# Block 1 of a two-block network on one Trainium2 core: where its modulation sums, token shift, norm weights and low weight parts are computed

## The chip, the cores and the metric

The kernel runs on one core of a Trainium2 chip. A core has TensorE for matrix products (PE in the profile, its weight loads PEld), VectorE (DVE), ScalarE (ACT), GpSimd (POOL), and SyncE (SP), which here issues most DMA transfers. Each engine takes its instructions strictly in its own order and waits on semaphores for the others. The metric is the device time of one execution in microseconds (us), the median of the runs.

## The reference, cut to what matters

Two blocks are computed on 512 tokens of 1024 channels, all in fp32. The change lies in the first; the second (attention, two MLPs, a gated recurrence) follows it and is not touched.

```
mod = silu(c) @ w_ada + b_ada              # shift, scale, gate
h = x * (1 + scale) + shift
p = h @ w_in
# branch A: u, v, gate = parts of p
v = layer_norm(gelu(v), ln_v_g, ln_v_b)    # per token, in 8 groups of 64 channels
v = einsum('gts,bcsgd->bctgd', w_m, v) + b_spatial   # mixes 128 tokens, causal
out_a = gelu(u) * v * silu(gate)
# branch B: r, k, v, gate, decay and rate inputs
p_b = p_b + mu * (prev_token(p_b) - p_b)   # token shift
... rwkv7 recurrence over 512 tokens, group norm, * silu(gate)
o = concat([out_a, out_b]) @ w_out
x = layer_norm(ALPHA * x + gate * o, ln_g, ln_b)
```

## The kernel before, in words

Every large product is made of three products of fp32r halves: a weight `raw` is cast to its upper part `wh` on ScalarE and the rest, `wl = raw - wh`, is subtracted (`wsplit`, L173); activations are split likewise into `aH` and `aL`. One chunk of output channels is then 8 steps of three matmuls (`mm3`, L181: the weight's and the activation's upper parts, and the two mixed products), 24 matmuls of 128x512 in all, summed in one PSUM bank.

Block 1 has three stages.

The **start loop** (L396 to L421) goes over eight chunks of input channels. For chunk k it forms shift and scale: `ada_acc` (L349) multiplies eight blocks of `w_ada` by silu(c) and adds them into two accumulators in turns (steps 0 and 1 start them, 2 to 7 add, step 8 adds the two), `modulated` (L379) sums the result over partitions with two matmuls against a column of ones, adds the bias into `mod`, turns x and applies them: ScalarE writes `h`, then its upper part `aH`, then `xa`, the scaled x for later. VectorE subtracts `aL`. TensorE multiplies chunk k with six blocks of `w_in`. The block is inside `ordered()`: each engine issues these elementwise instructions in the order of the program, and the matmuls have an order token too. The sums of chunk k+1 are formed while chunk k is multiplied.

The **mixing stage** runs a list written out by hand, `ORDER` (L41): products for k (`k`) and r (`r`) of four pairs of heads, `prep` in parts (`g`), the norm (`n`), transposed weights (`t`) and mixing (`m`) of branch A, the window products `lmat` (`l`), and steps of filling products (`f`). This order fixes TensorE's instructions; the elementwise instructions of the other engines are placed by a list scheduler with priorities. Two PSUM banks carry `mm`, three `sm`, two `mg`, one `po`. A product can start only when an older one has left its bank, and leaves it through `shift_evac` (L431): ScalarE copies the bank to `sh`, GpSimd subtracts neighbouring tokens, VectorE combines them with `mu`.

In the **inverse and window stage** VectorE inverts 32x32 blocks in 62 small dependent instructions (`inverse`, L742; `TV` and `bz` in the rows), the result goes through DRAM (`scT`), and eight windows of the recurrence follow, each starting with a product that needs it (`mg<-Tst,M`). TensorE fills the time of the inverse with the eight products of `ugate` (L654).

`pow_` (L242, shown as L245) is a power on GpSimd that all norms use.

Of the kernel before, what the change touches and what calls it, by code (L numbers as in the profile page):

```python
# [48 lines left out]
class Acts:  # L49
    """Channel-major activations split exactly into two float32r parts."""  # L50
# [11 lines left out]
class Kern:  # L62
# [30 lines left out]
    def psums(self, tags, keep=0):  # L93
        """PSUM banks, so many for each tag; the first pools may stay"""
# [62 lines left out]
    def wload(self, src, k, m, eng=None):  # L157
        """src: DRAM [k*128, m] -> raw tile view [128, k, m]"""
# [31 lines left out]
    def gemm(self, w, col0, acts, K, evac, idx, m=P, leng=None, tag="mm"):  # L190
        """one chunk of m output channels: psum[m, T] = w[:, col0:col0+m].T @ acts"""
# [9 lines left out]
    def gemm_halves(self, w, cols, acts, K, evac, idxs, then=None, tags=None):  # L201
        """chunks of output channels, the first half of the tokens of all of them before the second"""
# [10 lines left out]
    def split(self, src, hi, lo, g=None):  # L213
        """hi + lo = src * g, exactly split; src fp32 in SBUF"""
# [8 lines left out]
    def tokstat(self, acc_list, s=FULL, tag="sm"):  # L223
        """acc tiles [128, T] -> psum [128 tok, len * blocks] of the sums over partitions"""
# [7 lines left out]
    def bcast(self, *cols, tag="sm"):  # L232
        """[128 tok, blocks] each -> psum [128, blocks * 128] each, the same on every partition"""
# [14 lines left out]
    def consts(self):  # L248
# [22 lines left out]
                ("ln_g", r1("ln_g"), 8), ("ln_b", r1("ln_b"), 8)],  # L271
# [5 lines left out]
    def params(self, tag, rows_tile):  # L277
        """parameters, channel on partition: their loads and what turns them"""
# [22 lines left out]
    def block1(self):  # L301
# [10 lines left out]
        mod = self.cp.tile([P, 24], F32, tag="mod", name="mod")  # shift, 1 + scale, gate  # L312
# [6 lines left out]
        # what the output projection and its norm need again waits in DRAM  # L319
# [21 lines left out]
        def ada_load(pool, k, lo, n, bufs):  # L341
            """n blocks of w_ada, lo * 8 + k, (lo + 1) * 8 + k, .."""
# [6 lines left out]
        def ada_acc(acc, raw, steps=range(9)):  # L349
# [46 lines left out]
        with self.ordered():  # L396
            self.petoken = "start"
            ada_acc(cur[3], cur[1])
            w_ = self.wsplit(cur[2], 1, 6 * P, nc.gpsimd)
            h32 = modulated(0, cur[0], cur[3])  # L400
            for k in range(8):
                wh, wl = w_
                if k < 7:
                    cur = load(k + 1)
                    ada_acc(cur[3], cur[1], range(AS))
                self.tt(hL[k], h32, self.f(hH[k]), ALU.subtract)
                if k < 7:
                    ada_acc(cur[3], cur[1], range(AS, 9))
                for f in loads[2 * k : 2 * k + 2]:
                    f()  # L410
                for tb in range(NB):
                    s = slice(tb * P, (tb + 1) * P)
                    self.mm3(psv[tb], hH[k][:, s], hL[k][:, s], wh[:, 0, :T], wl[:, 0, :T], k == 0, k == 7)
                    if tb == SB and k < 7:
                        w_ = self.wsplit(cur[2], 1, 6 * P, nc.gpsimd)
# [26 lines left out]
        mk2 = b([P, 2, RC], "mk2")  # columns t of A (s < t) and of R (s <= t); rows s twice  # L442
# [5 lines left out]
        # rows (head, s), columns (head, t): s in the lower, t in the upper half of one head  # L448
# [6 lines left out]
        # -------- B branch: low-rank inputs of decay and in-context rate  # L455
# [3 lines left out]
        k00 = self.tl(pp, [P, T], "k0")  # L459
# [4 lines left out]
        hp = b_([P, 16], "hp")  # w0/2, a0/2, k_a/2, 1-k_a/2  # L464
# [6 lines left out]
        nc.gpsimd.memset(m64[:, :, 0:1], 0.0)  # L471
        ind2 = b_([P, 2], "ind2")
# [5 lines left out]
        def k_gemm(p):  # L478
            ks[p] = self.tl(pp, [P, T], "k0")
# [7 lines left out]
        def prep(p):  # L487
            """what a pair of heads brings to the windows, in parts that other products may come between"""
# [16 lines left out]
            nc.gpsimd.tensor_copy(out=PCt[p], in_=eP[:, :, RC])  # L505
# [1271 lines left out]
```

## Time and profile before

| | |
|---|---|
| median of 3 runs | 1627.69 us (1627.19 to 1629.02) |
| span of the profiled execution, first to last instruction | 1623.7 us |
| the profiled execution's own time | not recorded apart from its span; the median is 4.0 us above the span |
| TensorE, VectorE, ScalarE, GpSimd busy | 1554.1, 947.0, 704.4, 325.0 us |
| mean granted TensorE clock | 0.987 |

A row of the timeline gives the start in us, the time in us that the row's instructions cover, engine, line, operation, the tile written and the tiles read, shapes and types, the count, and in brackets how long the engine had been idle and what it waited for. An fp32 matmul against ones is two rows of the trace. A granted clock of 1.00 is the 2.4 GHz level, 0.50 the 1.2 GHz level.

### The profile page before, as it was taken

How to read it: one execution, taken by the hardware profiler on the slowest of the kernel's cores; microseconds unless marked ns; L12 is line 12 of the kernel's file. 1: busy time of each engine (PE TensorE's matmuls, PEld its weight loads, DVE VectorE, ACT ScalarE, POOL GpSimd, SP SyncE). 2: the span in 40 equal slices, each digit the busy share in tenths (PEclk: the TensorE clock that was granted, in tenths of full speed). 3: DMA queues.
4: the chain of work that ended last, by engine and by line, in shares of the span. 5: the costliest groups of instructions: out<-in, count | busy, mean ns of one | idle time of the engine just before them, and what ended most of it. 6: DMA issues, size and time to landing. Idle time of an engine off the chain costs nothing. (4 is left out here: it accounts for less than half of the span.)

```text
span 1623.7 us, 22045 instructions
## 1 busy us (share of the span) xinstructions
PE 1554.1 (96%) x8389; PEld 1317.7 (81%) x8389; DVE 947.0 (58%) x1651; ACT 704.4 (43%) x1217; POOL 325.0 (20%) x459
## 2 busy tenths in 40 slices
PE   5987979999999999999999999999999999999998
PEld 4766768889978899888888887888889988888886
DVE  7798595678667738233343456677754824343445
ACT  3533315655666645332232334666535523322331
POOL 4465631234310023000000032222313200000000
PEclk9998889999999999999999999999999999999999
DMA  9732445544123133333333232322213223231421
GB/s 290 219 96 82 75 130 144 176 139 112 52 69 91 33 111 90 93 92 102 91 93 102 80 102 66 103 66 66 71 47 105 91 79 115 64 120 65 120 88 52
DMA packets 272894, 161.70 MB, mean 100 GB/s; under 512 B 29465, under 2 KB 253316, under 8 KB 272788
## 3 DMA queue, kind: packets, MB, share of 16 engines
q1 hardware_dynamic: 271492, 157.33, 33.6%
q0 software_dynamic: 1152, 2.70, 0.5%
q8 instruction: 66, 1.08, 0.3%
q14 instruction: 40, 0.33, 0.1%
q10 hardware_dynamic: 144, 0.26, 0.1%
HBM read 147.42 MB, written 11.53 MB: 98 GB/s over the span
## 5 line engine op out<-in xcount | busy, mean ns | idle before, releaser
L123 DVE TENSOR_TENSOR wl<-raw,wh 128x1024 fp32r<-128x1024 f32 (+2 forms) x228 | 272.1, 1194 | 291.1 <-ACT wh L140 287.0
L140 ACT CAST wh<-raw 128x1024 fp32r<-128x1024 f32 (+3 forms) x244 | 242.6, 996 | 449.1 <-PE mm L143 354.2
L143 PE MATMUL mm<-bL,wh 128*128 128x512 f32 (+1 forms) x752 | 282.6, 378 | 1.0 <-DVE bL L133 1.0
L143 PE MATMUL mm<-bH,wl 128*128 128x512 f32 (+1 forms) x752 | 281.5, 377 | 0.0
L143 PE MATMUL mm<-bH,wh 128*128 128x512 f32 (+1 forms) x752 | 278.9, 378 | 0.1
L143 PE MATMUL mm<-aH,wh 128*128 128x512 f32 (+1 forms) x656 | 240.6, 369 | 11.2 <-DVE gt L133 7.0
L143 PE MATMUL mm<-aH,wl 128*128 128x512 f32 (+1 forms) x656 | 236.8, 362 | 1.5 <-DVE wl L123 1.5
L143 PE MATMUL mm<-aL,wh 128*128 128x512 f32 (+1 forms) x656 | 237.7, 363 | 0.0
L143 PEld LDWEIGHTS mm<-bL,wh 128*128 128x128 f32 x752 | 141.1, 188 | 29.0 <-DVE bL L133 1.8
L143 PEld LDWEIGHTS mm<-bH,wl 128*128 128x128 f32 x752 | 141.1, 188 | 27.4
L143 PEld LDWEIGHTS mm<-bH,wh 128*128 128x128 f32 x752 | 139.1, 188 | 28.4 <-ACT hg_vt L137 0.5
L143 PEld LDWEIGHTS mm<-aH,wh 128*128 128x128 f32 x656 | 125.1, 191 | 33.4 <-DVE gt L133 7.9
L143 PEld LDWEIGHTS mm<-aH,wl 128*128 128x128 f32 x656 | 125.1, 191 | 20.7 <-DVE wl L123 1.9
L143 PEld LDWEIGHTS mm<-aL,wh 128*128 128x128 f32 x656 | 125.5, 191 | 18.3 <-issue 0.7
L143 PE MATMUL mm<-wh,aH 128*128 128x512 f32 x288 | 113.5, 396 | 1.5 <-ACT aH L140 1.5
L143 PE MATMUL mm<-wh,aL 128*128 128x512 f32 x288 | 112.6, 393 | 0.0
L143 PE MATMUL mm<-wl,aH 128*128 128x512 f32 x288 | 112.5, 392 | 0.0
L140 ACT CAST aH<-t 128x512 fp32r<-128x512 f32 (+1 forms) x74 | 41.1, 564 | 75.7 <-DVE t L123 75.5
L123 POOL TENSOR_TENSOR mlpt<-mlpt,sq 128x256 f32<-128x256 f32 (+1 forms) x9 | 11.9, 1320 | 306.5 <-ACT sq L137 306.5
L245 POOL TENSOR_TENSOR mlpss<-mlpss,pwm 128x1 f32<-128x1 f32 x4 | 2.2, 547 | 321.8 <-DVE mlpss L128 321.8
L123 DVE TENSOR_TENSOR aL<-t,aH 128x512 fp32r<-128x512 f32 (+1 forms) x74 | 45.0, 617 | 36.2 <-ACT aH L140 36.2
L143 PEld LDWEIGHTS mm<-wh,aH 128*128 128x128 f32 x288 | 54.6, 190 | 12.8 <-ACT aH L140 1.9
(546 smaller groups left out, 2831.4 us busy)
## 6 DMA issues: line engine op xcount, KB each, us to landing
raw<-in_mlp_w_dram SPq DMA_DIRECT2D x128, 512.0 KB
raw<-in_hgrn_w_in_dram SPq DMA_DIRECT2D x32, 512.0 KB
raw<-in_w_in_dram SPq DMA_DIRECT2D x23, 512.0 KB
ada<-in_w_ada_dram SPq DMA_DIRECT2D x16, 512.0 KB
raw<-in_w_out_dram SPq DMA_DIRECT2D x10, 512.0 KB
raw<-in_w_ada_dram SPq DMA_DIRECT2D x8, 512.0 KB
raw<-in_mla_w_o_dram SPq DMA_DIRECT2D x8, 512.0 KB
raw<-in_hgrn_w_o_dram SPq DMA_DIRECT2D x8, 512.0 KB
```

The source lines that it names most:

```text
L123: self.st((eng or self.nc.vector).tensor_tensor(out=out, in0=a, in1=b, op=op))
L140: self.st(self.nc.scalar.copy(out=out, in_=in_))
L143: i = self.nc.tensor.matmul(out, l, r, start=start, stop=stop, **kw)
L245: self.nc.gpsimd.tensor_tensor(out=out, in0=a, in1=cst[: a.shape[0], :n], op=ALU.pow)
```

## The change

Nothing is computed differently but for rounding. In the start loop the first two steps of each sum move from VectorE to ScalarE, the addition of the two accumulators is left to TensorE, which now multiplies both by ones and adds them in PSUM, and the low part `wl` moves from GpSimd to VectorE. The token shift becomes `mu * p` on ScalarE and `(1 - mu) * p + shifted` on VectorE, read from PSUM. The gain of the norm in branch A is applied behind the mixing, and its bias is multiplied with the row sums of the mixing weights (eight more matmuls, `on64`) into `bsp`. Five smaller operations change engine: in `prep` the copies `PCt` and `rx` and the affine `kf` go to ScalarE, the product with `eP` to VectorE, and in `lmat` the mask of `LK` goes to VectorE; so do the low parts of `ugate`'s weights. The parameter loads go out three per chunk in place of two. Comments are removed as well.

```diff
-                if q < 2:
+                if q < 2 and first:
+                    first(acc[q], raw[:, q], AF.Copy, scale=sc[:, q : q + 1])
+                elif q < 2:
                     self.ts(acc[q], raw[:, q], sc[:, q : q + 1])
...
             for j in range(2):
-                self.mm(pa[:, j : j + 1], acc[0][:, j, :], self.ones[:, 0:1])
+                for q in range(2):
+                    self.mm(pa[:, j : j + 1], acc[q][:, j, :], self.ones[:, 0:1], q == 0, q == 1)
...
-                    ada_acc(cur[3], cur[1], range(AS))
+                    ada_acc(cur[3], cur[1], range(AS), self.act)
                 self.tt(hL[k], h32, self.f(hH[k]), ALU.subtract)
                 if k < 7:
-                    ada_acc(cur[3], cur[1], range(AS, 9))
-                for f in loads[2 * k : 2 * k + 2]:
+                    ada_acc(cur[3], cur[1], range(AS, 8))
+                for f in loads[3 * k : 3 * k + 3]:
...
-                        w_ = self.wsplit(cur[2], 1, 6 * P, nc.gpsimd)
+                        w_ = self.wsplit(cur[2], 1, 6 * P)
...
+        omu = b([P, 17], "omu")
+        self.ts(omu, self.pc("mu_b", 0, 17), -1.0, 1.0)
+        shs = [b([P, T + 1], f"sh{i}") for i in range(3)]
...
         def shift_evac(ps, mc, out, v3=False):
-            sh = self.tl(bp, [P, T + 1], "sh", bufs=2)
-            nc.gpsimd.memset(sh[:, 0:1], 0.0)
-            self.copy(sh[:, 1 : T + 1], ps)
-            d = self.tl(bp, [P, T], "shd", bufs=2)
-            self.tt(d, sh[:, 0:T], sh[:, 1 : T + 1], ALU.subtract, nc.gpsimd)
+            sh = shs[0]
+            shs.append(shs.pop(0))
+            self.act(sh[:, 1 : T + 1], ps, AF.Copy, scale=self.pc("mu_b", mc))
             o3 = lambda a: a.rearrange("p (c t) -> p c t", t=RC) if v3 else a
-            self.stt(out, o3(d), self.pc("mu_b", mc), o3(sh[:, 1 : T + 1]), ALU.mult, ALU.add)
+            self.stt(out, o3(ps), omu[:, mc : mc + 1], o3(sh[:, 0:T]), ALU.mult, ALU.add)
...
-            nc.gpsimd.tensor_copy(out=PCt[p], in_=eP[:, :, RC])
+            self.copy(PCt[p], eP[:, :, RC])
...
-            self.ts(kf, t2, hp[:, 8 + p : 9 + p], hp[:, 12 + p : 13 + p])
+            self.act(kf, t2, AF.Identity, scale=hp[:, 8 + p : 9 + p], bias=hp[:, 12 + p : 13 + p])
...
-            nc.vector.tensor_copy(out=rx.rearrange("p (n i) -> p n i", i=64), in_=rs.unsqueeze(2).to_broadcast([P, 2 * NB, 64]))
+            self.copy(rx.rearrange("p (n i) -> p n i", i=64), rs.unsqueeze(2).to_broadcast([P, 2 * NB, 64]))
...
-            self.tt(AR[p][:, :, 1, :], AR[p][:, :, 1, :], eP[:, :, 1 : RC + 1], ALU.mult, nc.gpsimd)
+            self.tt(AR[p][:, :, 1, :], AR[p][:, :, 1, :], eP[:, :, 1 : RC + 1], ALU.mult)
...
-            self.tt(LK[p][hf], LK[p][hf], at(mk2).unsqueeze(1).to_broadcast([P, 4, P]), ALU.mult, nc.gpsimd)
+            self.tt(LK[p][hf], LK[p][hf], at(mk2).unsqueeze(1).to_broadcast([P, 4, P]), ALU.mult)
...
+            ps = self.ptl("sm")
+            for g in range(8):
+                self.mm(ps[64 * (g % 2) : 64 * (g % 2) + 64, (g // 2) * P : (g // 2 + 1) * P], on64, wmT[:, g, :])
+            for j in range(4):
+                self.stt(bsp[:, j], ps[:, j * P : (j + 1) * P], self.pc("lnvb", j), bsp[:, j], ALU.mult, ALU.add)
             return wmT
...
-            v2 = vg.rearrange("p h i -> p (h i)")
-            self.tt(v2, v2, lng, ALU.mult, nc.gpsimd)
-            self.tt(v2, v2, lnb, ALU.add)
-            return v2
+            return vg.rearrange("p h i -> p (h i)")
...
-            yield from part_gemm(w_in, j * P, u_evac, nc.gpsimd)
-            yield from part_gemm(w_in, 1024 + j * P, g_evac, nc.gpsimd)
+            yield from part_gemm(w_in, j * P, u_evac)
+            yield from part_gemm(w_in, 1024 + j * P, g_evac)
```

The change moves instructions, too. The first place is ScalarE in the start loop, one round of chunks; `xa` closes one chunk, `wh` and `h` belong to the next, and `acc` are the new first steps of the sum after it. Before:

```order
L137 ACTIVATE xa_161<-sm_352 128x512
L140 CAST wh_402<-raw_378 128x768
L137 ACTIVATE h_81_415<-sm_410,mod 128x512
L140 CAST aH_126<-h_81_415 128x512
L137 ACTIVATE xa_161<-sm_410 128x512
L140 CAST wh_460<-raw_436 128x768
```

And now, on the same engine:

```order
L137 ACTIVATE xa_161<-sm_359 128x512
L137 ACTIVATE acc_75_389<-ada_381,sc 128x256
L137 ACTIVATE acc_76_390<-ada_381,sc 128x256
L140 CAST wh_409<-raw_385 128x768
L137 ACTIVATE h_81_424<-sm_419,mod 128x512
L140 CAST aH_126<-h_81_424 128x512
L137 ACTIVATE xa_161<-sm_419 128x512
```

The two steps stand behind `h`, `aH` and `xa` of the chunk before and ahead of `wh`. On VectorE the same sum's steps 2 to 6 come directly behind `mod`, ahead of `aL`, as they did.

The second place is the mixing stage: what empties the bank of the second product for k, `mm_766` before and `mm_770` now, into which the product after the next is summed. Before, that was ScalarE, in its queue:

```order
L137 ACTIVATE gsq_908<-vn_683 128x512
L137 ACTIVATE gsq_920<-vn_685 128x512
L140 CAST wh_954<-raw_952 128x1024
L140 COPY sh_791<-mm_766 128x512
L137 ACTIVATE ld_801<-sm_797,hp 128x512
```

Now VectorE reads the bank last, from its own queue, behind the norm of branch A (`vn`, `lw`) and a weight's low part (`wl`):

```order
L606 TENSOR_REDUCE lw_926<-gsq_930 128x8
L130 TENSOR_SCALAR lw_926<-lw_926 128x8
L123 TENSOR_TENSOR vn_699<-vn_699,lw_916 128x512
L123 TENSOR_TENSOR wl_939<-raw_936,wh_938 128x1024
L133 SCALAR_TENSOR_TENSOR k_123_763<-mm_770,omu,sh_653 128x512
L130 TENSOR_SCALAR ld_801<-ld_801 128x512
```

The bank is free when this `k` is written; before it was free when `sh` was.

The third place is VectorE in the inverse. Before, its instructions `bz` and `TV` followed each other, with only the exits of the filling products (`gt`) between:

```order
L123 TENSOR_TENSOR TV_1582<-TV_1582,bz_1583 128x24x8
L123 TENSOR_TENSOR bz_1583<-XT_1581,TV_1582 128x207
L123 TENSOR_TENSOR TV_1582<-TV_1582,bz_1583 128x23x9
L123 TENSOR_TENSOR bz_1583<-XT_1581,TV_1582 128x220
L123 TENSOR_TENSOR TV_1582<-TV_1582,bz_1583 128x22x10
```

Now the low parts of the filling products' weights stand among them:

```order
L123 TENSOR_TENSOR TV_1551<-TV_1551,bz_1552 128x24x8
L123 TENSOR_TENSOR wl_1794<-raw_1791,wh_1793 128x1024
L123 TENSOR_TENSOR bz_1552<-XT_1550,TV_1551 128x207
L123 TENSOR_TENSOR TV_1551<-TV_1551,bz_1552 128x23x9
L123 TENSOR_TENSOR bz_1552<-XT_1550,TV_1551 128x220
```

Six such subtractions now lie between the inverse's first and last instruction, and the exits of three gate products instead of two. TensorE's own order is the same but for the added products with ones and `on64`.

## Rows read from the trace of the kernel before

**Rows 1.** The page's first line.
```profile
span 1623.7 us, 22045 instructions
```

**Rows 2.** Busy time by stretch: mixing stage, inverse, windows, two microseconds in them.
```profile
core 0: us, PE busy (x) PEld busy (x) DVE busy (x) ACT busy (x) POOL busy (x), PEclk, DMA share, GB/s
62.00:183.00 121.00, 104.50 (x553) 84.99 (x553) 91.29 (x123) 48.44 (x73) 69.10 (x74) 0.89 0.41 109
183.00:240.00 57.00, 47.90 (x199) 38.46 (x197) 47.02 (x95) 13.04 (x17) 24.11 (x18) 0.94 0.48 128
240.00:340.00 100.00, 96.43 (x654) 83.12 (x654) 61.17 (x153) 54.87 (x123) 23.98 (x38) 0.98 0.49 143
242.00:244.00 2.00, 2.00 (x11) 1.59 (x10) 0.00 (x0) 0.36 (x1) 0.80 (x2) 0.50 0.24 36
```

**Rows 3.** Timeline, VectorE, one round of the start loop.
```profile
33.37 0.16 DVE L123 TENSOR_TENSOR mod<-sm,bada 128x2 f32<-128x2 f32 x1 [0.76 <-PE sm L143]
...
33.98 2.06 DVE L133 SCALAR_TENSOR_TENSOR acc<-ada,sc,acc 128x256 f32<-128x256 f32 x5
35.96 0.68 DVE L123 TENSOR_TENSOR aL<-h,aH 128x512 fp32r<-128x512 f32 x1
36.57 0.48 DVE L133 SCALAR_TENSOR_TENSOR acc<-ada,sc,acc 128x256 f32<-128x256 f32 x1
37.08 1.93 DVE L123 TENSOR_TENSOR acc<-acc,acc 128x256 f32<-128x256 f32 x1
39.77 0.16 DVE L123 TENSOR_TENSOR mod<-sm,bada 128x2 f32<-128x2 f32 x1 [0.76 <-PE sm L143]
```

**Rows 4.** Timeline, ScalarE, the same round.
```profile
33.86 0.78 ACT L137 ACTIVATE h<-sm,mod 128x512 f32<-128x512 f32 x1 [3.75 <-PE sm L149]
34.67 0.62 ACT L140 CAST aH<-h 128x512 fp32r<-128x512 f32 x1
35.20 0.59 ACT L137 ACTIVATE xa<-sm 128x512 f32<-128x512 f32 x1
35.69 0.83 ACT L140 CAST wh<-raw 128x768 fp32r<-128x768 f32 x1
```

**Rows 5.** Timeline, TensorE, the end of the round before.
```profile
30.95 0.40 PE L143 MATMUL mm<-wl,aH 128*128 128x512 f32 x1
31.18 0.40 PE L143 MATMUL mm<-wh,aL 128*128 128x512 f32 x1
32.75 0.58 PE L143 MATMUL sm<-ones,acc 128*128 128x1 f32 x4 [1.17 <-DVE acc L123]
```

**Rows 6.** Timeline, GpSimd, the same round.
```profile
36.59 2.14 POOL L123 TENSOR_TENSOR wl<-raw,wh 128x768 fp32r<-128x768 f32 x1 [3.31 <-ACT wh L140]
```

**Rows 7.** Timeline, TensorE, its longest waits from 60 to 245 us.
```profile
119.03 1.39 PE L143 MATMUL sm<-wmT,vn 128*64 128x128 f32 x6 [4.10 <-DVE mx L123]
...
159.40 2.07 PE L143 MATMUL sm<-AR,BK 64*128 64x128 f32 x8 [6.39 <-ACT res L140]
...
208.76 0.80 PE L143 MATMUL mm<-aH,wh 128*128 128x512 f32 x1 [6.39 <-DVE gt L133]
...
239.84 1.08 PE L143 MATMUL mg<-Tst,M 128*128 128x64 f32 x8 [2.06 <-DMA Tst<-scT]
```

**Rows 8.** Timeline, three engines: the second product for k and its two exits.
```profile
72.30 0.39 PE L143 MATMUL mm<-aH,wh 128*128 128x512 f32 x1
...
79.58 0.58 ACT L140 COPY sh<-mm 128x512 f32<-128x512 f32 x1
...
90.58 0.74 DVE L133 SCALAR_TENSOR_TENSOR k<-shd,pb,sh 128x512 f32<-128x512 f32 x1
```

**Rows 9.** Timeline, VectorE, a weight's low part.
```profile
58.13 1.21 DVE L123 TENSOR_TENSOR wl<-raw,wh 128x1024 fp32r<-128x1024 f32 x1
```

**Rows 10.** The power on GpSimd, instructions of tile rs (ns min/median/max).
```profile
L245 POOL TENSOR_TENSOR rs<-rs,pwm x4: 1637/1862/2090, 100.2 to 159.7; 128x8 f32<-128x8 f32 x4
```

**Rows 11.** Timeline, VectorE, two instructions of the inverse.
```profile
194.94 1.24 DVE L123 TENSOR_TENSOR bz<-XT,TV 128x87 f32<-128x87 f32 x1
...
200.19 2.48 DVE L123 TENSOR_TENSOR TV<-TV,bz 128x192 f32<-128x192 f32 x1
```

More of the change, by code (lines that the diff above doesn't have):

```diff
@@ L347, in ada_load, with ada_acc @@
             return raw
-        def ada_acc(acc, raw, steps=range(9)):
+        def ada_acc(acc, raw, steps=range(9), first=None):
             for q in steps:
-                if q < 2:
+                if q < 2 and first:
+                    first(acc[q], raw[:, q], AF.Copy, scale=sc[:, q : q + 1])
+                elif q < 2:
                     self.ts(acc[q], raw[:, q], sc[:, q : q + 1])
@@ L397, in block1 @@
             self.petoken = "start"
-            ada_acc(cur[3], cur[1])
-            w_ = self.wsplit(cur[2], 1, 6 * P, nc.gpsimd)
+            ada_acc(cur[3], cur[1], range(8), self.act)
+            w_ = self.wsplit(cur[2], 1, 6 * P)
             h32 = modulated(0, cur[0], cur[3])
@@ L414, in block1 @@
                     if tb == SB and k < 7:
-                        w_ = self.wsplit(cur[2], 1, 6 * P, nc.gpsimd)
+                        w_ = self.wsplit(cur[2], 1, 6 * P)
                         h32 = modulated(k + 1, cur[0], cur[3])
@@ L429, in block1 @@
         b_ = lambda s, n, dt=F32: pp.tile(s, dt, tag=n, name=n, bufs=1)
-        def shift_evac(ps, mc, out, v3=False):
-            sh = self.tl(bp, [P, T + 1], "sh", bufs=2)
-            nc.gpsimd.memset(sh[:, 0:1], 0.0)
-            self.copy(sh[:, 1 : T + 1], ps)
-            d = self.tl(bp, [P, T], "shd", bufs=2)
-            self.tt(d, sh[:, 0:T], sh[:, 1 : T + 1], ALU.subtract, nc.gpsimd)
+        omu = b([P, 17], "omu")
+        self.ts(omu, self.pc("mu_b", 0, 17), -1.0, 1.0)
+        shs = [b([P, T + 1], f"sh{i}") for i in range(3)]
+        for z in shs:
+            nc.gpsimd.memset(z[:, 0:1], 0.0)
+        def shift_evac(ps, mc, out, v3=False):
+            sh = shs[0]
+            shs.append(shs.pop(0))
+            self.act(sh[:, 1 : T + 1], ps, AF.Copy, scale=self.pc("mu_b", mc))
             o3 = lambda a: a.rearrange("p (c t) -> p c t", t=RC) if v3 else a
-            self.stt(out, o3(d), self.pc("mu_b", mc), o3(sh[:, 1 : T + 1]), ALU.mult, ALU.add)
+            self.stt(out, o3(ps), omu[:, mc : mc + 1], o3(sh[:, 0:T]), ALU.mult, ALU.add)
         mk2 = b([P, 2, RC], "mk2")
@@ L458, in block1 @@
         self.act(tw[0:64, :], tw[0:64, :], AF.Tanh)
-        k00 = self.tl(pp, [P, T], "k0")
+        k00 = self.tl(pp, [P, T], "k0", bufs=3)
         shift_evac(psk, 4, k00)
@@ L471, in block1 @@
         nc.gpsimd.memset(m64[:, :, 0:1], 0.0)
+        on64 = b_([P, 64], "on64")
+        nc.gpsimd.memset(on64, 1.0)
         ind2 = b_([P, 2], "ind2")
@@ L478, in k_gemm @@
         def k_gemm(p):
-            ks[p] = self.tl(pp, [P, T], "k0")
+            ks[p] = self.tl(pp, [P, T], "k0", bufs=3)
             self.gemm(w_in, 2048 + p * P, h, 8, lambda i, ps, s: shift_evac(ps, 4 + p, ks[p]), 0)
@@ L565, in a_load @@
         def a_load():
-            lng = a_([P, T], "lng")
-            lnb = a_([P, T], "lnb")
-            nc.sync.dma_start(out=lng, in_=I["ln_v_g"].rearrange("a b -> (a b)").partition_broadcast(P))
-            nc.sync.dma_start(out=lnb, in_=I["ln_v_b"].rearrange("a b -> (a b)").partition_broadcast(P))
             bsp = a_([P, 4, P], "bsp")
@@ L575, in a_load, with a_turn @@
             nc.gpsimd.affine_select(out=wsp, in_=wsp, compare_op=ALU.is_ge, fill=0.0, base=0, pattern=[[0, 8], [-1, P]], channel_multiplier=1)
-            return lng, lnb, bsp, wsp
-        def a_turn(wsp):
+            return bsp, wsp
+        def a_turn(wsp, bsp):
             wmT = a_([P, 8, P], "wmT")
@@ L713, in block1 @@
             elif op == "A":
-                lng, lnb, bsp, wsp = a_load()
+                bsp, wsp = a_load()
             elif op == "n":
-                vn = [a_norm(tb, lng, lnb) for tb in range(NB)]
+                vn = [a_norm(tb) for tb in range(NB)]
             elif op == "t":
-                wmT = a_turn(wsp)
+                wmT = a_turn(wsp, bsp)
             elif op == "m":
```

6 lines of the change are left out of this document (3 added, 3 removed).

## The prediction

> **What bounds the kernel now.** I read the page's head for the span, 1623.7 us [rows 1], then the busy times by stretch, then the timeline of each stretch of block 1, because the change touches nothing behind it. The median of the runs, 1627.69 us, lies 4.0 us above the span; the sum is made in the span, and 4.0 us are added. Of this kernel about 0.2% (3.3 us) can be told from no change.
>
> TensorE is busy nearly always, so a microsecond is won only where TensorE stops waiting or runs at its higher clock. In the mixing stage it is busy 104.50 of 121 us: 16.5 us of waits, at a mean granted clock of 0.89 [rows 2]. A mean of 0.89 between the levels 1.00 and 0.50 is 0.11 x 121 / 0.5 = 26.6 us at 1.2 GHz; some 6.5 of them are themselves waits, so about 20 busy us take twice as long and cost 10 us. In the inverse stage the waits are 57 - 47.9 = 9.1 us, the windows after it are almost full [rows 2]. The longest waits are 4.10, 6.39 and 6.39 us, for VectorE or for ScalarE behind it, and 2.06 us for the inverse's way through DRAM [rows 7].
>
> In the start loop one round takes 39.77 - 33.37 = 6.40 us [rows 3]. VectorE sets it: its last instruction, the addition of the two accumulators, takes 1.93 us although half of the 0.68 us of `aL` would do for its size [rows 3]; it ends with GpSimd's `wl`, 36.59 + 2.14 [rows 6]. TensorE waits 1.17 us for it [rows 5].
>
> **The change part by part. Start loop.** The addition goes, and with it GpSimd's hold. But the loop gets another chain. The two first steps now stand on ScalarE behind `h`, `aH` and `xa`, and VectorE's steps 2 to 6, which need them, still stand ahead of `aL`. Counted from `mod` at 0: ScalarE's `h` starts at 0.49, `aH` at 1.30, `xa` at 1.83, and the next slot is at 35.69 - 33.37 = 2.32 [rows 4]. There the first step runs. It is not in the trace; 512 columns take 0.62 and 768 take 0.83 [rows 4], so 256 take about 0.41, with the hand-over 0.45 (between 0.3 and 0.62): 2.77. Five steps of VectorE, 2.06, then `aL`, 0.68 [rows 3]: 5.51. TensorE has finished the chunk before by then and waits for `aL`: its third product of the next chunk needs it, and four products at 0.23 apart (31.18 - 30.95) [rows 5] end at 6.43. Then eight rows against ones instead of four: four take 0.58 and `mod` follows 33.37 - 32.75 = 0.62 behind their start [rows 3, 5], so 0.62 + 0.58: the next `mod` at 7.63. That is 1.2 us more per round. `wl` on VectorE, 768 columns at under 1.21 us [rows 9], fits into the time of those products and costs nothing; without that cover it would be 0.95. From `mod` of chunk 2 to that of chunk 7 there are five rounds: +6.0. The first two rounds run at TensorE's lower speed, where the four products, the eight rows and the turns behind them take twice as long: I put +2.3 each, +4.6. The first sum, with no chunk before it, ends about 1.0 earlier. Start loop: **+9.6 us** (bounds: -4, if the waits for ScalarE were hidden and only the hold went, and +19 by the second rival).
>
> **Mixing stage.** All of its GpSimd holds go but those of the power. VectorE gains twelve products of 512 columns and three `wl` (12 x 0.68 + 3 x 1.21 = 11.8 at most) and loses four additions of the bias, four `kf` and four `rx` (up to 12 x 0.68 = 8.2) [rows 3, 9]; of its 91.29 busy us [rows 2] far more is holding. Its queue comes through earlier, and the waits (16.5) and the slow stretches (10) can go: -26.5. What comes in their place:
>
> - The bank of the second product for k. It starts at 72.30; 24 products of it, one microsecond of small ones and 24 of the next at 0.23 bring TensorE to 84.4, where the product into the same bank begins. Before, ScalarE freed it at 80.2. Now VectorE's `k` frees it, which ended at 91.3 [rows 8]; by the new order a scan, `kf` and the bias addition are no longer ahead of it, some 2.3 us. So a wait of 89.0 - 84.4 = 4.6 us (0 to 6.9), and about 1.5 us at the lower clock after it. It then is the stage's longest.
> - `on64`: sixteen rows at 0.58 per four [rows 5], and its weights come straight from ScalarE: 2.2 us.
> - `lmat` waits for `sm` banks, whose exits now queue behind masks on VectorE: 2 us (0 to 6).
> - The power stays on GpSimd, eight times about 1.64 to 2 us [rows 10]. A small instruction of the inverse took 1.24 beside a GpSimd product, several times its size's worth [rows 11]; if a quarter of the eight catch a two-input instruction, that is 1.7 us on TensorE (0 to 13).
>
> Together 12.0, and the stage comes out at **-14.5 us** (-26 to 0).
>
> The Trainium skill, page "SBUF — State Buffer", section "Who interferes with whom", says that a VectorE instruction with two SBUF inputs and a GpSimd instruction that reads SBUF exclude each other for a whole instruction, whatever its size. The trace agrees with the hold (1.93 beside 2.14), and by the rule alone the eight powers, which read SBUF, would still hold VectorE for up to 8 x 1.64 = 13.1 us and the sum would end at +6.5 instead of -4.9. No row shows a power that held that much, so I do not take it.
>
> **Inverse.** Five of its additions were held by a `wl` on GpSimd, as the 2.48 us row of 192 columns, at most 2.1 too long each; three by a product, as the 1.24 us row, by 1.0 [rows 11]. The five go, -10; the three stay. Six `wl` come onto VectorE, 6 x 1.21 = +7.3 [rows 9], and one more pair of exits. It nets about **-2 us** (-6 to +4). The wait at 208.76 shrinks, but TensorE then is ahead of the inverse, and the wait of 2.06 at 239.84 grows to some 6 us.
>
> **Windows.** After 2.06 us at 239.84 the clock was 0.50 [rows 2, 7]; after a longer wait it stays there longer: **+2 us** (0 to 5). Nothing else changes there.
>
> Sum: +9.6 - 14.5 - 2.0 + 2.0 = -4.9 us; 1623.7 - 4.9 + 4.0 = 1622.8, so **1623 us**.
>
> **Rivals.** (1) *The new waits are hidden:* the scheduler's VectorE is at k's bank in time, and `lmat`, the power and the windows cost nothing; 4.6 + 1.5 + 2 + 1.7 + 2 = 11.8 less, 1611 us. For it speaks that VectorE's queue loses its holds exactly there; against it, `k` stands behind the whole norm of branch A. (2) *Slower: the start loop loses the clock.* Its wait grows from 1.17 to about 2.1 us per round, with thin work against ones behind it. After 2.06 us with thin work the clock was 0.50 at 242 [rows 2, 7], and with 1.17 the products were 0.23 us apart [rows 5]. If it falls in the loop, four products, eight rows and the turns take 1.5 us more in each of six rounds: +9 us, 1632. It decides against the change as soon as four of the six rounds run low. (3) *VectorE becomes the bound of the mixing stage:* thirteen banks now wait for an in-order queue, and half of the stage's gain stays away: +7, 1630, no change. (4) That GpSimd's holds are not what the 1.93 us are is excluded by their common end.
>
> **Chances.** Forecast 0.45, with its own range 1616 to 1630; rival 1 0.2, rival 2 0.2, rival 3 0.15. Of the forecast 0.28 lies faster than 1624.4, 0.13 within 1624.4 to 1631.0 and 0.04 above; rival 1 is all faster; rival 2 is 0.01, 0.05 and 0.14; rival 3 0.03, 0.07 and 0.05. Faster 0.52, same 0.25, slower 0.23. The range reaches over rivals 1 and 2 to most of their width: 1608 to 1634.
>
> **What would show it.** In the start loop rounds of 7.6 us, VectorE waiting for ScalarE's `acc`, TensorE for `aL`. At the third product after r of pair 0 a wait of 4 to 5 us for VectorE's `k`. No wait above 2 us from there to the last `lmat`, clock 1.00. At the first window a wait of about 6 us for the inverse. I am wrong if the rounds are 6.4 us or shorter, or if the mixing stage still takes 115 us.

## The result, and the profile after

The changed kernel takes 1643.17 us (median of 4 runs, 1642.81 to 1644.86), the kernel before 1627.44 us in the same comparison: a ratio of 1.0098, 95% interval 1.0083 to 1.0112. It is slower by 15.7 us, where 1623 us and a range of 1608 to 1634 were forecast.

The page's first line [rows 1], and the stretches of [rows 2], of the changed kernel (stretch, its length, busy time of TensorE, its weight loads, VectorE, ScalarE, GpSimd; granted clock, DMA share, GB/s):

```profile
span 1641.2 us, 22090 instructions
```

```profile
62.00:183.00 121.00, 110.02 (x607) 89.34 (x606) 86.87 (x141) 61.16 (x94) 25.22 (x32) 0.92 0.41 113
183.00:240.00 57.00, 48.00 (x200) 38.84 (x198) 42.15 (x99) 13.60 (x17) 6.42 (x8) 0.94 0.59 137
240.00:340.00 100.00, 91.12 (x598) 78.33 (x599) 57.16 (x142) 52.03 (x112) 19.19 (x32) 0.95 0.45 131
372.00:388.00 16.00, 12.37 (x83) 11.87 (x82) 10.39 (x20) 4.95 (x12) 4.90 (x42) 0.79 0.37 109
```

GpSimd does a third of what it did in the mixing stage, 25.22 us against 69.10. TensorE is busier in the same stretch, but the first 7 us of it now belong to the start loop. Taken from the last `mod` to the last `lmat` product (both below), TensorE stood idle for 16.5 of 121.2 us before and for 10.6 of 112.2 us after, at a granted clock of 0.89 and 0.92. Busy time doesn't say where the microseconds went, though. For that I took instructions that both programs have and read how much later each stands in the second trace. Three of them close the start loop (the last `mod`), the mixing stage (the last `lmat` product) and the windows (a product of the output projection). In the kernel before:

```profile
59.27 0.15 DVE L123 TENSOR_TENSOR mod<-sm,bada 128x2 f32<-128x2 f32 x1
...
180.55 0.71 PE L143 MATMUL sm<-AR,BK 64*128 64x128 f32 x4 [0.28 <-ACT res L140]
...
346.46 0.38 PE L143 MATMUL mm<-aH,wh 128*128 128x256 f32 x1 [0.15 <-ACT wh L140]
```

And in the changed kernel:

```profile
69.00 0.15 DVE L123 TENSOR_TENSOR mod<-sm,bada 128x2 f32<-128x2 f32 x1
...
181.33 0.71 PE L143 MATMUL sm<-AR,BK 64*128 64x128 f32 x4 [1.48 <-ACT res L140]
...
353.60 0.39 PE L143 MATMUL mm<-aH,wh 128*128 128x256 f32 x1 [0.16 <-ACT wh L140]
```

With the first window's product (239.84 before, [rows 7]; 244.57 after, below) and the two spans this gives the account by stage:

| stage | its end is later by | the stage itself | forecast |
|---|---|---|---|
| start loop | 9.7 | +9.7 | +9.6 |
| mixing stage | 0.8 | -8.9 | -14.5 |
| inverse | 4.7 | +3.9 | -2 |
| windows | 7.1 | +2.4 | +2 |
| all that follows | 17.5 | **+10.4** | **0** |

The table compares one execution of each kernel. Their spans are 17.5 us apart and the medians 15.7. In every run for which both are on record, an execution's own time lies 1.7 us above its span; by that, an estimate, the profiled execution of the kernel before was about 2 us faster than its median, and the sum should have added 1.7 us in place of 4.0.

The largest single loss lies where the diff touches no line. The long waits of TensorE in the changed kernel, which answer to [rows 7]:

```profile
82.28 0.79 PE L143 MATMUL po<-aH,wh 128*128 128x512 f32 x1 [5.95 <-DVE tw L133]
...
209.71 0.79 PE L143 MATMUL mm<-aH,wh 128*128 128x512 f32 x1 [6.60 <-DVE gt L133]
...
244.57 0.66 PE L143 MATMUL mg<-Tst,M 128*128 128x64 f32 x2 [6.97 <-DMA Tst<-scT]
...
379.32 0.58 PE L143 MATMUL mm<-aH,mla_cH 128*128 128x256 f32 x1 [2.63 <-ACT mla_cH L140]
...
479.80 0.50 PE L143 MATMUL mm<-wh,mla_cH 128*128 128x512 f32 x1 [2.24 <-ACT mla_vt L140]
```

Of the waits of before, 119.03 (4.10) is gone and 159.40 (6.39) has shrunk below 2 us, as forecast; 208.76 (6.39) stayed, and three new ones stand at 82, 379 and 480 us.

**Start loop.** VectorE, one round, as in [rows 3]:

```profile
45.89 0.16 DVE L123 TENSOR_TENSOR mod<-sm,bada 128x2 f32<-128x2 f32 x1 [0.81 <-PE sm L143]
48.74 2.08 DVE L133 SCALAR_TENSOR_TENSOR acc<-ada,sc,acc 128x256 f32<-128x256 f32 x5 [2.69 <-ACT acc L137]
50.73 0.69 DVE L123 TENSOR_TENSOR aL<-h,aH 128x512 fp32r<-128x512 f32 x1
...
51.73 0.95 DVE L123 TENSOR_TENSOR wl<-raw,wh 128x768 fp32r<-128x768 f32 x1
53.50 0.16 DVE L123 TENSOR_TENSOR mod<-sm,bada 128x2 f32<-128x2 f32 x1 [0.81 <-PE sm L143]
```

The two steps on ScalarE that it waits for, in one row, as they stand behind `xa` [rows 4], and TensorE's wait for `aL`:

```profile
48.22 0.90 ACT L137 ACTIVATE acc<-ada,sc 128x256 f32<-128x256 f32 x2
```

```profile
51.47 0.50 PE L143 MATMUL mm<-wh,aL 128*128 128x512 f32 x1 [1.94 <-DVE aL L123]
```

The round is 7.61 us. VectorE stands idle 2.69 us behind `mod`, until ScalarE has done `h`, `aH`, `xa` and the first of the two steps; `aL`, queued behind the five steps that follow, ends 5.53 us after `mod` (5.51 in the forecast).

**The wait at 82 us.** The first product for r goes into a bank that `tw` has to leave. The store on GpSimd's queue, and `tw` on VectorE, which waits for it:

```profile
71.48 0.95 POOL L423 DMA_DIRECT2D xaD<-xa  x1 [57.23 <-ACT xa L137]
...
81.47 0.75 DVE L133 SCALAR_TENSOR_TENSOR tw<-sm,omu,sh 128x512 f32<-128x512 f32 x1 [2.91 <-DMA xaD<-xa]
```

In the kernel before the same `tw` waited for the same store, but the bank had been emptied by then, by ScalarE's copy:

```profile
66.08 0.59 ACT L140 COPY sh<-sm 128x512 f32<-128x512 f32 x1 [2.98 <-PE sm L143]
...
71.20 0.75 DVE L133 SCALAR_TENSOR_TENSOR tw<-shd,pb,sh 128x512 f32<-128x512 f32 x1 [2.01 <-DMA xaD<-xa]
```

`tw` lies in memory that `xa` held, and the one store of all of `xa` lands about 10 us after the last chunk. Before, that wait held up an instruction that nobody needed yet; now it holds a PSUM bank.

**The inverse.** Before, SP's queue ahead of it, and its first and last instruction on VectorE:

```profile
173.88 6.41 SPq L749 DMA_DIRECT2D XT<-scL  x12
180.63 0.42 SPq L555 DMA_DIRECT2D scL<-res  x1
182.46 0.38 SPq L555 DMA_DIRECT2D scL<-L  x1
...
185.86 1.50 SPq L749 DMA_DIRECT2D XT<-scL  x4
...
191.65 0.19 DVE L123 TENSOR_TENSOR bz<-XT,TV 128x31 f32<-128x31 f32 x1 [7.44 <-DMA raw<-in_w_in_dram]
...
230.82 0.19 DVE L123 TENSOR_TENSOR TV<-TV,bz 128x31 f32<-128x31 f32 x1
```

After:

```profile
176.16 6.65 SPq L757 DMA_DIRECT2D XT<-scL  x12
182.91 0.99 SPq L161 DMA_DIRECT2D raw<-in_w_in_dram  x1
184.01 1.58 SPq L564 DMA_DIRECT2D scL<-res  x1
185.69 0.79 SPq L564 DMA_DIRECT2D scL<-L  x1
...
191.48 1.50 SPq L757 DMA_DIRECT2D XT<-scL  x4
...
197.47 0.19 DVE L123 TENSOR_TENSOR bz<-XT,TV 128x31 f32<-128x31 f32 x1 [7.89 <-DMA XT<-scL]
...
233.57 0.19 DVE L123 TENSOR_TENSOR TV<-TV,bz 128x31 f32<-128x31 f32 x1
```

The work on VectorE became shorter, 36.3 us from first to last instruction against 39.4. But it starts 5.8 us later although TensorE's last `lmat` product is only 0.8 us later. The two stores to `scL` go out 3.4 us later, for two reasons in SP's queue: the twelve loads of `XT` ahead of them begin 2.3 us later, and a weight's load now stands between. The four loads behind the stores then go out 5.6 us later. From the last `TV` to the first window it is 10.8 us instead of 8.8: the first load of `Tst` goes out 5.3 us behind the last `TV`, at 239.01, where it was 4.0 us before.

**Behind the windows.** ScalarE before; `mla_cH` is where the last weights of the output projection are kept, the first of their six casts:

```profile
363.65 1.14 ACT L140 CAST mla_cH<-raw 128x512 fp32r<-128x512 f32 x2 [1.86 <-DMA raw<-in_w_out_dram]
```

And after, with VectorE's last use of `gbn`, the bonus and bias of the group norm:

```profile
377.14 0.68 DVE L123 TENSOR_TENSOR gsh<-gsh,gbn 128x512 f32<-128x512 f32 x1
...
377.85 0.30 ACT L140 CAST aH<-gsh 128x128 fp32r<-128x128 f32 x1 [0.18 <-DVE gsh L123]
...
378.65 2.17 ACT L140 CAST mla_cH<-raw 128x512 fp32r<-128x512 f32 x4
```

The casts, which used to wait for nothing but their weight, now come in a row behind the last group norm. TensorE's wait of 2.63 us is the smaller part of the price: from 372 to 388 us it is busy for 12.37 of 16 us, at a granted clock of 0.79 (its row is above), where it was busy throughout at 1.00 before. The addresses in the built programs say why (bytes within a partition):

```
tile              before             after
gbn (last ones)   159520 - 161568    161440 - 163488
AR, pair 0        161696 - 165792    163616 - 167712
mla_cH0           162656 - 164704    162656 - 164704
```

`mla_cH0` lies at the same place in both. Before, it lay on `AR` alone, whose last reader is a product of the last window; now its first 832 bytes lie on `gbn`, and its cast has to come behind the last instruction that reads `gbn`. Block 1's pool has become 1920 bytes smaller (the four tiles of 2080 and 2048 bytes for `sh` and `shd` went, three `sh` and one `omu` came), and everything stacked below it has moved up.

### The profile page after: what moved, and what is told of

The parts are those of the page before. It is cut to its first block, busy times and chain, and to the rows that moved or that the text cites. A ratio compares the mean times of both kernels' runs of the same rounds, so it can differ in the third digit from the quotient of the medians.

```text
span 1641.2 us, 22090 instructions
## 1 busy us (share of the span) xinstructions
PE 1563.6 (95%) x8437; PEld 1325.3 (81%) x8437; DVE 920.1 (56%) x1648; ACT 718.2 (44%) x1245; POOL 243.5 (15%) x395
## 5 line engine op out<-in xcount | busy, mean ns | idle before, releaser
L123 DVE TENSOR_TENSOR wl<-raw,wh 128x1024 fp32r<-128x1024 f32 (+3 forms) x244 | 286.7, 1176 | 310.8 <-ACT wh L140 306.9
L143 PEld LDWEIGHTS mm<-aL,wh 128*128 128x128 f32 x656 | 125.2, 191 | 18.4 <-issue 0.5
L143 PEld LDWEIGHTS mm<-wh,aL 128*128 128x128 f32 x288 | 55.2, 192 | 23.9 <-DVE aL L123 12.6
L123 DVE TENSOR_TENSOR aL<-t,aH 128x512 fp32r<-128x512 f32 (+1 forms) x74 | 45.1, 618 | 36.9 <-ACT aH L140 36.9
L143 PEld LDWEIGHTS mm<-wl,aH 128*128 128x128 f32 x288 | 55.3, 192 | 11.3
```

The source lines that it names most:

```text
L123: self.st((eng or self.nc.vector).tensor_tensor(out=out, in0=a, in1=b, op=op))
L143: i = self.nc.tensor.matmul(out, l, r, start=start, stop=stop, **kw)
```

## The experiments

Twelve kernels, each timed in 4 to 11 runs beside the kernel before. "After" below is the changed kernel at 1643.17 us.

| label | start | median us | ratio to before, 95% interval |
|---|---|---|---|
| a_pad | after | 1634.15 | 1.0043 (1.0031 to 1.0056) |
| b_shift | before | 1633.74 | 1.0041 (1.0028 to 1.0053) |
| a_store | after | 1638.36 | 1.0068 (1.0056 to 1.0081) |
| a_first | after | 1624.82 | 0.9986 (0.9976 to 0.9995) |
| a_tw | after | 1639.42 | 1.0070 (1.0057 to 1.0083) |
| a_low | after | 1649.75 | 1.0131 (1.0113 to 1.0149) |
| a_first_pad | after | 1619.24 | 0.9947 (0.9934 to 0.9960) |
| a_first_pad_tw | after | 1614.47 | 0.9922 (0.9907 to 0.9937) |
| b_loop | before | 1636.34 | 1.0055 (1.0043 to 1.0068) |
| b_join | before | 1624.96 | 0.9978 (0.9969 to 0.9987) |
| best_scl | after | 1606.29 | 0.9866 (0.9852 to 0.9879) |
| a_scl | after | 1633.24 | 1.0038 (1.0024 to 1.0051) |

**a_pad and b_shift: the addresses.** a_pad gives block 1's pool its 1920 bytes back:

```diff
         for z in shs:
             nc.gpsimd.memset(z[:, 0:1], 0.0)
+        nc.gpsimd.memset(b([P, 480], "pad")[:, 0:1], 0.0)
```

> The changed kernel with one unused tile of 1920 bytes per partition added to block 1's pool, so that all tiles behind it lie where they lay before. Theory (layout): the change made that pool 1920 bytes smaller, the tile mla_cH0 now lies partly on the gbn tile of the last group norm, and so the six casts of the last weights of the output projection stand behind that norm on ScalarE; of the 17.3 us that TensorE is late at the end, the 10.2 us that appear after 354 us go away: 1633 us (1631 to 1636), no wait of 2.63 us at the first product with mla_cH. Rival (late entry): the casts are late only because block 1 ends late; then it stays at 1643 us.

b_shift does the reverse to the kernel before, whose block 1 stays as it is; 1120 bytes in the pool of `mla_cH0` move that tile down to 161536, so that 32 bytes of it lie on `gbn`:

```diff
         self.mla_rope = x_("COS"), x_("SIN")
+        self.nc.gpsimd.memset(self.mla_x.tile([P, 280], F32, tag="pad", name="pad")[:, 0:1], 0.0)
```

> The kernel before with 1120 bytes added to the pool of mla_cH0, which moves that tile down until 32 bytes of it lie on gbn; block 1 itself is unchanged. Theory (layout): slower by 7 to 10 us, 1635 to 1638 us, with the same waits at the first product with mla_cH as in the changed kernel. Rival (late entry): block 1 ends when it did, nothing is late, 1627.5 us.

a_pad is 9.0 us faster than after, and ScalarE's first cast is back ahead of the group norm; TensorE is busy throughout from 372 to 388 us (columns as in the result):

```profile
371.17 1.14 ACT L140 CAST mla_cH<-raw 128x512 fp32r<-128x512 f32 x2 [1.61 <-DMA raw<-in_w_out_dram]
```

```profile
372.00:388.00 16.00, 16.00 (x136) 15.88 (x135) 13.07 (x30) 7.60 (x17) 5.50 (x6) 1.00 0.51 146
```

b_shift loses 6.5 us on the kernel before and has the same wait as after, to 0.03 us:

```profile
374.09 0.39 PE L143 MATMUL mm<-aH,mla_cH 128*128 128x256 f32 x1 [2.66 <-ACT mla_cH L140]
```

Both directions agree, and the rival (late because block 1 is late) is out: in b_shift TensorE reaches the output projection 2.1 us late, and is 7.6 us late right behind that wait. So 9.0 of the 15.7 us come from where tiles lie. a_pad wins them wholly behind the windows: its first product of the output projection stands at 353.45 us, against 353.60 in after. The order repeats: in a_store, a_first, a_tw, a_low and a_scl, which lack the 1920 bytes, four casts come in a row too; in the three combinations, which have them, and in b_loop and b_join they come in pairs that wait for their weights. In a_pad TensorE still loses 1.7 us behind the windows, at the copy `mla_vt` (a wait of 2.00 us in place of 2.24) and after it; what moves that copy isn't settled.

**a_store and a_tw: the wait at 82 us.** a_store takes the one store of `xa` apart:

```diff
+                self.st(nc.gpsimd.dma_start(out=xaD[k], in_=xa[:, k]))
...
-            self.st(nc.gpsimd.dma_start(out=xaD.rearrange("k p t -> p k t"), in_=xa))
```

> The changed kernel with xa stored chunk by chunk (eight stores of 256 KB) in place of one store of 2 MB behind the loop. Theory (store): TensorE's wait of 5.95 us at the first r product is VectorE's tw, which waits for the memory of xa until the one store has landed; with eight stores the wait is under 1 us, and the 6 us with some of the low clock behind it are won: 1635 us (1633 to 1638). Rival (absorbed): what is won there is waited for again before the inverse, since VectorE and the way through DRAM set its end: 1641 to 1643 us.

It wins 4.8 us, between the two ranges, but the wait does not vanish: TensorE still waits 4.40 us for `tw`. That size says little by itself, as the same wait is 3.57 us in a_scl, 4.36 in a_pad and 5.48 in a_low, where nothing was edited there. What shows the new cause is the order on VectorE. The wait for the store, now over at 75.6 us, passes to another instruction, and `tw` has been placed behind the norm of branch A, where it starts at 79.66:

```profile
75.63 0.58 DVE L128 TENSOR_SCALAR hp<-pb 128x4 f32<-128x4 f32 x3 [3.00 <-DMA xaD<-xa]
...
79.66 0.75 DVE L133 SCALAR_TENSOR_TENSOR tw<-sm,omu,sh 128x512 f32<-128x512 f32 x1
```

a_tw therefore gives `tw`, and the k beside it, memory that never was `xa`'s:

```diff
-        tw = b_([P, T], "tw")
+        tw = V[3]
...
-        k00 = self.tl(pp, [P, T], "k0", bufs=3)
+        k00 = V[2]
```

> The changed kernel with the first two results of the token shift, tw and k of pair 0, written into the tiles V3 and V2 (free until much later) in place of memory that xa held. Theory (memory): in the run with eight stores tw no longer had to wait for the store, but stood behind the norm of branch A in VectorE's queue, and TensorE still waited 4.40 us; with no wait for the store at all, tw comes right after its ScalarE step, TensorE's wait falls from 5.95 to under 1.5 us and the total by 5 to 8 us: 1635 to 1638 us. Rival (absorbed): TensorE comes to the inverse earlier and waits there instead, 1640 to 1643 us.

```profile
81.20 0.50 PE L143 MATMUL po<-aH,wh 128*128 128x512 f32 x1 [0.95 <-DVE V L133]
...
102.03 0.50 PE L143 MATMUL mm<-aH,wh 128*128 128x512 f32 x1 [2.92 <-DVE k L133]
```

The wait falls from 5.95 to 0.95 us, so its cause is shown: `tw` now waits for ScalarE alone. The wait for the bank of the second product for k, which the prediction had named, appears with 2.92 us; in the changed kernel the earlier wait had covered it. The total falls by 3.7 us, less than expected, but this trace can't say what the wait is worth. From the last `mod` to the last `lmat` product it takes 112.3 us in both kernels, because in this execution the granted clock was 0.72 from 70 to 80 us, against 0.92 in after. The pair a_first_pad and a_first_pad_tw below shows it better. There the wait falls from 5.54 to 0.94 us, the clock from 65 to 75 us rises from 0.68 to 1.00, and the stage becomes 3.2 us shorter, 107.6 us against 110.7:

```profile
63.60 0.50 PE L143 MATMUL po<-aH,wh 128*128 128x512 f32 x1 [0.94 <-DVE V L133]
```

**a_first: the start loop's steps.** The edit, in both calls:

```diff
-                    ada_acc(cur[3], cur[1], range(AS), self.act)
+                    ada_acc(cur[3], cur[1], range(AS))
```

> The changed kernel with the first two steps of each sum back on VectorE; the joined sums and the low parts on VectorE stay. Theory (chain): the rounds of 7.6 us come from the steps behind h, aH and xa on ScalarE; they fall to 6.4 us or a little less, the loop's 9.7 us go away and 1 to 2 us more: 1632 us (1630 to 1635). Rival (ones rows): the eight rows against ones and the low part on VectorE carry the longer round; rounds stay above 7.2 us, 1639 us or more.

```profile
32.40 0.16 DVE L123 TENSOR_TENSOR mod<-sm,bada 128x2 f32<-128x2 f32 x1 [0.85 <-PE sm L143]
...
37.80 0.16 DVE L123 TENSOR_TENSOR mod<-sm,bada 128x2 f32<-128x2 f32 x1 [0.85 <-PE sm L143]
```

Rounds of 5.40 us, not 6.4: 18.4 us are won, 14.35 of them in the loop (its last `mod` stands at 54.65). TensorE is busy 40.00 of the 40 us from 20 to 60. The chain through ScalarE is confirmed, and the ones rows are not the cause. The theory missed that with that chain gone the joined sums and the low part on VectorE together take the round below the 6.4 us of before, which it had taken as the floor.

**b_loop and b_join: the loop alone.** Both put the changed start loop into the kernel before, b_loop with the first steps on ScalarE as in the change, b_join with them on VectorE:

```diff
-                self.mm(pa[:, j : j + 1], acc[0][:, j, :], self.ones[:, 0:1])
+                for q in range(2):
+                    self.mm(pa[:, j : j + 1], acc[q][:, j, :], self.ones[:, 0:1], q == 0, q == 1)
...
-                        w_ = self.wsplit(cur[2], 1, 6 * P, nc.gpsimd)
+                        w_ = self.wsplit(cur[2], 1, 6 * P)
```

> The kernel before with the start loop of the change alone: first steps on ScalarE, joined sums, low parts on VectorE; the rest as before. Theory (carried): rounds of 7.6 us, and the 9.7 us that they cost in the loop arrive whole at the end, since every engine of the mixing stage starts from it: 1637 us (1635 to 1638). Rival (absorbed): the mixing stage's waits of 16.5 us take up half or more of it, 1632 us or less.

> The same with the first steps on VectorE. Theory (carried): rounds of 5.4 us with TensorE busy throughout, 4.6 us won in the loop and kept: 1623 us (1621 to 1625). Rival (store): what follows waits for the store of xa, whose landing is set by the last xa and 10 us of transfer, and gives 2 us or more back: 1625 to 1627 us.

The loss is carried: +8.3 us by the medians (in the profiled run, the slowest of its five, the last `mod` is 10.9 us late and the end 12.6). The gain isn't: the loop ends 4.9 us early, and a wait of 3.79 us for ScalarE's `sh` follows at 90 us in the old mixing stage; by the medians 3.0 us remain, in the profiled run, the slowest of its eleven, none. b_join's time lies inside the range of its first theory, but half of the gain is gone, and not for the rival's reason: the store isn't what takes it back. Taking the steps off ScalarE wins 11.4 us with the old token shift behind the loop (b_join against b_loop) and 18.4 us with the new one (a_first against after).

**a_low: the low parts in the inverse.** They go back to GpSimd:

```diff
-            yield from part_gemm(w_in, j * P, u_evac)
+            yield from part_gemm(w_in, j * P, u_evac, nc.gpsimd)
```

(and the same for `g_evac`).

> The changed kernel with the low parts of the weights of ugate back on GpSimd. Theory (holds): they held VectorE longer than the 7.3 us that they now cost it there; the inverse takes 39 us again in place of 36.3 from its first to its last instruction, the first window is 2 to 3 us later: 1645 to 1646 us. Rival (queue): on VectorE they wait for their upper parts (4.4 us of idle time) and stop the inverse; on GpSimd the first window is 2 us or more earlier, 1641 us or less.

Slower by 6.6 us on after, in the direction of the first theory, but not for its reason. The inverse takes 36.3 us (194.90 to 231.25) with the low parts on either engine, because the exchange is even: in after, six low parts of 1.22 to 1.23 us lie in it and three pairs of bank exits; in a_low, four instructions held to between 2.38 and 2.45 us, and two pairs. The kernel before had five held ones, two pairs and an exit of the old token shift, 39.4 us in all. The first window is 1.5 us earlier than in after (243.03 against 244.57). The loss comes after it, in waits of the first two windows for VectorE's `Psb` (1.55 and 3.74 us). For the second of them VectorE stood idle in front of a low part whose weight came late, with `Psb` queued behind:

```profile
256.22 1.23 DVE L123 TENSOR_TENSOR wl<-raw,wh 128x1024 fp32r<-128x1024 f32 x1 [10.62 <-ACT wh L140]
```

The inverse of a_low also says something of its start. No weight stands ahead of the stores to `scL` there, and it still starts 14.7 us behind the last `lmat` product (180.22), against 16.1 in after and 11.1 before. So the weight is worth some 1.5 us of the 5.0, an estimate from single traces; the rest, as far as these traces tell, is the later `XT` loads and their landing.

**a_scl: the stores to scL.** They are issued from ScalarE's queue in place of SP's:

```diff
-            nc.sync.dma_start(out=scL[:, p, cs], in_=LB[p][hf][:, :, 0:RC])
+            nc.scalar.dma_start(out=scL[:, p, cs], in_=LB[p][hf][:, :, 0:RC])
```

> The changed kernel with the stores to scL issued from ScalarE's queue, nothing else. In the best version this edit won 8 us: 1.7 us at the first window and 5.8 us of a stall in the second, where a weight came late from SP's queue; the changed kernel shows no such stall. Theory (start of the inverse): the inverse, which starts at 197.5 us in the changed kernel and at 191.7 us before, starts 4 to 5 us earlier, the first window 3 to 5 us earlier, and the total falls by as much: 1638 to 1640 us. Rival (not SP): the start stays within 1 us of 197.5, 1642 us or more.

```profile
189.47 0.19 DVE L123 TENSOR_TENSOR bz<-XT,TV 128x31 f32<-128x31 f32 x1 [2.87 <-DMA XT<-scL]
```

```profile
232.02 0.74 PE L143 MATMUL mg<-Tst,M 128*128 128x64 f32 x5 [1.22 <-DMA Tst<-scT]
```

9.9 us are won, above what was expected. The inverse starts 11.1 us behind the last `lmat` product (189.47 - 178.36), as before the change (191.65 - 180.55), against 16.1 in after. That is 5.0 us, for both reasons given above, as the stores no longer stand in that queue. 3.0 more are there already at that product, where the wait for `tw` came out at 3.57 us; the first store to `scL` comes only at 142.9 us, so the edit can hardly have done this. The rest up to the 12.6 us at the first window comes from the inverse itself (33.4 us, with five low parts and two pairs of exits in it) and from its way back through DRAM (9.2 us). This execution was the fastest of five, 13.1 us below after's by the spans. The size of the effect at its own place was forecast; where the rest of the 9.9 us comes from is not shown.

**The combinations.** a_first_pad puts the steps back and the 1920 bytes in, a_first_pad_tw adds V3 and V2, best_scl the stores.

> Both single edits that won: first steps back on VectorE, and the 1920 bytes. Theory (they add): 1624.8 - 9.0 = 1616 us (1614 to 1618), rounds of 5.4 us and no wait at the first product with mla_cH. Rival (shared): both win the same slack; 1620 us or more.

> The same with tw and k of pair 0 in V3 and V2 as well. Theory (memory): the wait of 6.58 us for tw at 68 us goes to under 1.5 us and most of it is kept: 1608 to 1612 us. Rival (absorbed): 1614 to 1617 us, with a longer wait at the first window or before it.

> The version with all three edits (first steps back, 1920 bytes, V3 and V2), and the stores to scL issued from ScalarE's queue in place of SP's. Theory (queue): the inverse starts 5.8 us later behind the last lmat than before because the last two stores stand in SP's queue behind twelve loads and a weight; they are issued 2 to 4 us earlier, the inverse starts as much earlier: 1611 to 1612.5 us. Rival (landing): the loads of XT, not the stores, take the time, or TensorE is not waiting for the inverse there; 1614 to 1615 us.

The four alone win 18.4, 9.0, 3.7 and 9.9 us on after, 41.0 together; best_scl wins 36.9. In the combination the steps give 18.4, the 1920 bytes 5.6, V3 and V2 4.8 and the stores 8.2 us: the second gives less than alone, the third more. best_scl is the version that beats both, 1606.29 us, ratio 0.9866 to the kernel before.

a_first_pad missed its 1616 us by 3.2, so not all of the slack was separate. a_first_pad_tw came out at 1614.47 us, in its rival's range, although the wait itself went. best_scl won 8.2 us where 2 to 3.5 were expected: the inverse starts 5.0 us earlier, of which 1.7 reach the first window, and a wait of 2.75 us in the second window, behind a weight that came late, is gone; at the first product of the fourth window it is 7.6 us ahead.

## Why the prediction was wrong

The step that failed is the first one: I read "the timeline of each stretch of block 1, because the change touches nothing behind it", and the sum had no term behind the windows. 10.4 us were lost there. The change touches nothing behind block 1 in the code, but it changes the sizes of tiles, and these set the addresses of all that is stacked on the same side of the memory. The new order on ScalarE could be read from the programs before any run: the six casts stand behind `aH<-gsh` and up to three more `raw<-res`. I compared the order only at places that the diff names. a_pad and b_shift show this step from both sides: 9.0 us given back, 6.5 us lost.

**Mixing stage, -14.5 forecast, -8.9 measured.** The steps "what comes in their place" named the bank of the second product for k, with 4.6 us. The same reasoning held for every bank that leaves through the token shift, and the first of them is `tw`'s: a wait of 5.95 us. Its cause is shown by a_tw, and its worth, 3.2 us of the stage, is best read in a_first_pad_tw. The k wait exists (2.92 us in a_tw) but was covered. From there on what went was as forecast: no wait above 1.6 us to the last `lmat` product. A second term was too large: I let the 10 us of slow stretches go ("clock 1.00") but for 1.5. The clock rose only from 0.89 to 0.92, and was 0.73 from 82 to 88 us, behind the `tw` wait, and 0.69 from 160 to 170. By the prediction's own reckoning that leaves 0.08 x 112 / 0.5 = 18 us at 1.2 GHz, an estimate, where there were 26.6. How the missing 5.6 us divide between the two is open.

**Inverse, -2 forecast, +3.9 measured.** The work on VectorE came out near the forecast, 3.1 us shorter, and for its reasons: the five held instructions went, and six low parts (7.35 us in all, 7.3 forecast) and a pair of exits came. I put at nothing where the inverse starts (5.0 us later behind the last `lmat` product) and its way back (2.0 us longer): I had counted what VectorE gains and loses, and not what else moves in SP's queue. a_scl, which takes the stores out of it, gives the 5.0 us back; a_low says that the weight's load is the smaller part of them. The wait of 6.97 us at the first window, forecast as "some 6", agrees by luck: the wait at 208.76 that was to feed it did not shrink (6.60 us), and the inverse came late instead.

**Start loop, +9.6 forecast, +9.7 measured.** Right in mechanism and in size, by a_first and b_loop, and also part by part: first sum -1.1 (forecast -1.0), first two rounds +4.25 (+4.6), five rounds +6.6 (+6.0). **Windows, +2:** +2.4.

Summed in spans: 22.4 us between the -4.9 us forecast and +17.5: 10.4 behind block 1, 5.6 in the mixing stage, 5.9 in the inverse, 0.5 in the other two. The sign did not hang on the addresses alone, as a_pad (+0.43%) is slower than before too. Of the single edits to the changed kernel only a_first comes out ahead of the kernel before (0.9986): the loop's steps, whose cost I knew, were outweighed in the sum by the -14.5 us that did not come in full. None of the signs of being wrong came true (rounds of 7.61 us, a stage of 112 us where 115 was the mark): they all lay ahead of the places where most was lost.

Of the rivals, the first did not happen. The second (the loop loses the clock) happened in small part: one round behind the start, from 37.83 to 45.89 us, took 8.06 us at a granted clock of 0.81; the rest of the loop's loss is the forecast's chain. The third is near in size, 5.6 us of the stage's gain stayed away, but not as described: as far as shown one bank held it, for the memory of its output, and not thirteen in an in-order queue. Without the wait for the one store the queue alone still held that bank, for 4.40 us in a_store.

## What to carry to other kernels

When a change alters the size or number of tiles, compare the addresses and the instruction order of the whole program, not of the part that was edited: 1920 bytes cost 9 us in a stage that nobody touched. When the reader of a PSUM bank moves to another engine, list every bank that it empties and everything its output waits for, memory included; a wait that was harmless on an output becomes a wait on the bank. And an in-order queue that carries both weight loads and a store that a chain waits for is worth splitting: here one word won 8 to 10 us.

## What was unexpected in the hardware

A power on GpSimd did not hold VectorE. From 96.69 to 99.94 us GpSimd ran two powers in the changed kernel; under the second, VectorE ran two instructions with two inputs from SBUF:

```profile
96.69 3.25 POOL L245 TENSOR_TENSOR lw<-lw,pwm 128x8 f32<-128x8 f32 x2 [2.46 <-DVE lw L130]
```

```profile
98.37 0.69 DVE L123 TENSOR_TENSOR vn<-vn,lw 128x512 f32<-128x512 f32 x1 [0.61 <-POOL lw L245]
98.98 1.22 DVE L123 TENSOR_TENSOR wl<-raw,wh 128x1024 fp32r<-128x1024 f32 x1
```

They took 0.69 and 1.22 us, as they do with GpSimd idle. The other way round a hold is possible: a power that began at 108.08 us, under a `wl` of 107.91 to 109.13, took 2.56 us, where the shortest take 1.64. If that was a hold, it was of the power and not of VectorE. The prediction kept 1.7 us on TensorE for holds of VectorE.

The rule that it weighed (the Trainium skill, page "SBUF — State Buffer", section "Who interferes with whom": such a pair excludes each other for a whole instruction) is not borne out for VectorE beside a running power; the measurement decides.

The same store to `scL` stood for 0.42 us in SP's queue before, for 1.58 us after, behind a weight's load, and for 1.03 us in a_low, where no weight stood ahead of it; what sets this isn't settled.
